# A pace of 0.56 instead of 0.46 for the S5 set-up in the last two token-major stages, and one more step in the mLSTM gates

## The chip, the cores and the metric

One core of a Trainium2 chip runs the whole program. Its engines work side by side, each through its own instruction queue in a fixed order, and wait for one another by semaphores: PE (TensorE, the matmuls), DVE (VectorE), ACT (ScalarE), POOL (GpSimd), and SP, which issues most of the DMA transfers. PE writes into eight PSUM banks, each of which another engine must read out before PE may use it again. The metric is the device time of one execution in microseconds (us), the median of several; lower is better.

## The reference, cut to what matters

One layer: an input projection of 1024 tokens, three mixers on its column groups (S5, mLSTM, SSD), an output projection and a LayerNorm.

```python
h = jnp.einsum('bld,dn->bln', x, w_in[l])          # 1024 x 2048 times 2048 x 6676
(s5_u, s5_z, ml_qk, ml_v, ml_i, ml_f, ml_o, ml_z, ssd_xbc, ssd_dt, ssd_z) = split_in(h)
y_s5 = s5_mixer(s5_u, ...) * silu(s5_z)            # diagonal complex state space, 32 groups x 64 states
y_ml = mlstm_mixer(q, k, ml_v, ml_i, ml_f, ml_o, ...) * silu(ml_z)   # gated matrix memory, 4 heads
y_ssd = rms_norm(ssd_mixer(...) * silu(ssd_z), ssd_norm_g)
out = jnp.einsum('bln,nd->bld', concatenate([y_s5, y_ml, y_ssd]), w_out[l])
x = layer_norm(DEEPNORM_ALPHA * x + out, ln_g[l], ln_b[l])
```

In `s5_mixer` the matrices that depend on the parameters alone (`lam_bar`, `b_bar`, the powers of `lam_bar`) can be formed before any token is known: that is the S5 set-up. In `mlstm_mixer` the running maximum of the gates, `m_row`, is needed for `exp(-m_row)` in the denominator: that is what the second edit moves.

## The kernel before

Every float32 operand is split into a high and a low part (`split`, L170 to L172: ACT casts the high part, DVE subtracts it for the low part), and each product is three matmuls: high by high, high by low, low by high.

The first part of the program, `block`, computes some column groups of the input projection by a recursive two-by-two scheme with seven products numbered 1 to 7. It has a token-major part (tokens on the partitions) in five stages, (1), (2), (5, 6), (3, 7) and (4). In each stage there are three column groups g = 0, 1, 2, of 512, 404 and 512 columns; each product of a group takes four units u, and one unit is 24 matmuls, which finish four PSUM banks named `b<i><g><t>` (product, group, token tile t) after the fourth unit. In stages (1), (2), (3, 7) and (4) all four banks come from one pool of four, `pj`: the next group writes the same four banks. In units 0 and 3 the matmuls run tile by tile, so that the banks finish, and are needed again, one after the other. `evac_t` reads a finished bank out with the additions of L1298 on DVE (tiles `e...`, named like the banks); product 7 has two such additions for a bank.

A column-major part follows (`b<i>c<g>`, L1443 to L1445), then for each half of the tokens the stage `half` with the projections for mLSTM and SSD and the mixers themselves, and at last `outproj`.

Work that is not on this main line is written as Python generators and handed to `Background`. Each unit ends with a `tick`, which adds the rate of the first generator in the list to an accumulator and runs one step of the generator (up to its next `yield`) for each whole number reached. The S5 set-up, `s5_setup`, is one such generator with 29 steps: 12 of small arithmetic, then two steps for each of eight blocks `sb`, and a last one. The first step of a block makes `s5lb`, `s5ob` (six 128x512 DVE products with helpers `s5l2`, `s5o2`) and writes `s5ob` to DRAM; the second makes `s5ta` (three more, with helper `s5tb`), writes it out, and calls `read_out(sb-1)`: four PE transposes `s5R` and four matmuls `s5K` of the tile `s5lb`, an ACT copy `s5rr`, a DVE addition `s5kb`, and two more writes. They use the other PSUM pool, `mx`. The set-up runs at rate 0.31 up to stage (3, 7), then at the rate that the diff changes; what is left after the last stage is run at once by `bg.finish(setup)`.

By these rates, of the 84 ticks of the token-major part (stage (3, 7) is ticks 49 to 72, stage (4) 73 to 84), 13 steps are done at tick 48. With 0.46 step 29 falls on tick 83; with 0.56 on tick 77, and the generator is closed at tick 79. The accumulator then passes 0.38 on to the next generator, the S5 mixer `s5_mix`, where it was 0.58.

The order in which steps are called is not the order of the queues: a scheduler between this code and the engines places the instructions of all steps by priorities and expected readiness. So the queues themselves are shown below.

In `half`, the generator `pre` runs `gates`, `cumulate` and `ml_gates` at rate 1.5. `ml_gates` ends with a part behind two yields: the four PE transposes `mg0mt` (L608) of the running maximum `mg0m`, which a DVE scan (L589) makes, and the ACT exponential of it. The main line at that place is `proj_c`, the products `qk0_0p`, `qk0_1p`, `qk0_2p`, each 48 matmuls with two weight tiles (`w125` and `w126` for the second, `w127` and `w128` for the third). Behind `pre` the generators `ml_mix`, `ml_finish` and `ssd_super` run.

Of the kernel before, what the change touches and what calls it, by code (L numbers as in the profile page):

```python
# [39 lines left out]
def hybrid_trunk(ctx: ExitStack, tc: tile.TileContext, a: dict, out: bass.AP, dbg=None):  # L40
# [15 lines left out]
    def gt(name, shape=(P, HT), dtype=F32):  # L56
        return gp.tile(list(shape), dtype, name=name, tag="g")

    def pm(name):
        return mx.tile([P, HT], F32, name=name, tag="mx")  # L60
# [106 lines left out]
    bg = Background()  # L167
# [417 lines left out]
    def ml_gates(h, G, NC, b, lf, ir, res):  # L585
        n = f"mg{h}"

        m = gt(n + "m", (4, HT))
        dve.tensor_tensor_scan(out=m, data0=lf, data1=ir, initial=mcar, op0=ALU.add, op1=ALU.max)  # L589
        mst = sp.tile([4, 4], F32, name=n + "mst", tag="mst")  # L590
        pool.tensor_copy(out=mst[:, 0:1], in_=mcar)
        pool.tensor_copy(out=mst[:, 1:4], in_=m[:, P - 1:3 * P:P])
        pool.tensor_copy(out=mcar, in_=m[:, HT - 1:HT])
        A = gt(n + "A", (4, HT))
        dve.tensor_tensor(out=A, in0=b, in1=m, op=ALU.subtract)
        sync.dma_start(out=rowd[h][12:16], in_=A)
        A2 = gt(n + "A2", (4, HT))
        ms = mst.unsqueeze(2).to_broadcast([4, 4, P])
        dve.tensor_tensor(out=A2.rearrange("p (c k) -> p c k", k=P), in0=A.rearrange("p (c k) -> p c k", k=P), in1=ms, op=ALU.add)
        sync.dma_start(out=rowd[h][16:20], in_=A2)  # L600

        Bj = sp.tile([P, 4, 4], F32, name=n + "Bj", tag="mBj")
        dve.tensor_tensor(out=Bj, in0=G[:, :, 16:20], in1=NC[:, :, 32:36], op=ALU.add)
        yield
        yield
        mt = pm(n + "mt")
        for c in range(4):
            pe.transpose(mt[:, 4 * c:4 * c + 4], m[:, c * P:(c + 1) * P], ident[0:4, 0:4])  # L608
        em = sp.tile([P, 16], F32, name=n + "em", tag="mem")
        act.activation(out=em, in_=mt[:, 0:16], func=AF.Exp, scale=-1.0)  # L610
        res += [Bj, em]
# [608 lines left out]
    def aside_1():  # L1220

        for u in range(4):
            c = Chain(xq(0, 0, u), (P, 2, HT), f"xc{u}")
            c.mix(xq(1, 0, u), sub, False, xs[u][7])
            yield

    def aside_2(X5):

        for u in range(4):
            c = Chain(xq(1, 0, u), (P, 2, HT), f"xd{u}")  # L1230
            c.mix(xq(1, 1, u), add)
            X5.put(c.r)
            yield
            c.mix(xq(0, 0, u), sub, False, xs[u][6])
            yield

    def aside_3():

        for u in range(4):
            yield  # L1240
            c = Chain(xs[u][6], (P, 2, HT), f"xe{u}")
            c.mix(xq(0, 1, u), sub, True, xs[u][3])
            yield
            yield

    def aside_4():

        for u in range(4):
            yield
            yield  # L1250
            c = Chain(xq(1, 0, u), (P, 2, HT), f"xf{u}")
            c.mix(xq(1, 1, u), add, False, xs[u][5])
            yield
# [31 lines left out]
    def block():  # L1285
# [78 lines left out]
        def unit(i, X, g, u, ps, w):  # L1364
            wh, wl = w
            N = GN[g]
            order = [(t, k) for t in range(4) for k in range(2)] if u == 3 or u == 0 and (i, g) != (1, 0) else [(t, k) for k in range(2) for t in range(4)]
            for t, k in order:
                K = 2 * u + k
                s_h, s_l = X.h[u][:, k, t * P:(t + 1) * P], X.l[u][:, k, t * P:(t + 1) * P]  # L1370
                pe.matmul(ps[t][:, 0:N], lhsT=s_h, rhs=wh[:, k, :], start=(K == 0), stop=False)
                pe.matmul(ps[t][:, 0:N], lhsT=s_h, rhs=wl[:, k, :], start=False, stop=False)
                pe.matmul(ps[t][:, 0:N], lhsT=s_l, rhs=wh[:, k, :], start=False, stop=(K == 7))  # L1373
                if K == 7:
                    evac_t(i, g, t, ps[t])
            tick()

        def banks(i, g, p):
            return [p.tile([P, HT], F32, name=f"b{i}{g}{t}", tag="pj" if p is pj else "mx") for t in range(4)]
# [6 lines left out]
        def ahead(sg, g, i, u):  # L1386

            if sg == (1,) and g == 1:
                ops[2].load(u)
            elif sg == (2,) and g == 2:  # L1390
                ops[6].load(u)
            elif sg == (5, 6) and (g, i) == (2, 6):
                ops[3].load(u)
                ops[7].load(u)
            elif sg == (3, 7) and (g, i) == (2, 3):
                ops[4].load(u)
            elif sg == (4,) and g == 1:
                cops[5].load(u)
            elif sg == (4,) and g == 2:
                cops[6].load(u)  # L1400

        for sg in STAGES:
            if sg == (2,):
                aside.append(aside_2(ops[5]))
            if sg == (5, 6):
                aside.append(aside_3())
            if sg == (3, 7):
                aside.append(aside_4())
                bg.q = [(q, 0.46) for q, _ in bg.q]
            for g in range(3):  # L1410
                if sg == (5, 6):
                    ps = {5: banks(5, g, pj), 6: banks(6, g, mx)}
                    for u in range(4):
                        w = [W.next(), W.next()]
                        for i, w_ in zip(sg, w):
                            unit(i, ops[i], g, u, ps[i], w_)
                        ahead(sg, g, 6, u)
                else:
                    for i in sg:
                        ps = banks(i, g, pj)  # L1420
                        for u in range(4):
                            if (i, g) == (1, 0):
                                first.load(u)
                            unit(i, ops[i], g, u, ps, W.next())
                            ahead(sg, g, i, u)
                if sg == (1,) and g == 0:
                    aside.append(aside_1())
# [52 lines left out]
    def half(h, X, Xn):  # L1480
# [4 lines left out]
        def pre():  # L1485
            G = Gs[:, h]
            DT, LC = gates(h, G)
            yield
            yield
            NC, b, lf, ir = cumulate(h, LC)  # L1490
            gx.extend([DT, NC])
            yield
            yield from ml_gates(h, G, NC, b, lf, ir, mlg)
# [117 lines left out]
    with tc.tile_pool(name="gb", bufs=NGB) as gp, tc.tile_pool(name="rb", bufs=NRB) as rw, tc.tile_pool(name="zp", bufs=NZ) as zp:  # L1611

        warm = gt("warm", dtype=BF16)
        dve.memset(warm, 0.0)
        wps = mx.tile([P, HT], F32, name="warmp", tag="mx")
        for _ in range(NWARM):
            pe.matmul(wps, lhsT=warm[:, 0:P], rhs=warm, start=True, stop=True)
        X[0] = block()
# [101 lines left out]
```

## Time and profile before

| quantity | value |
|---|---|
| time, median of 3 runs (lowest to highest) | 1613.33 us (1608.36 to 1613.99) |
| the profiled execution, its own time | 1613.81 us |
| its span, first to last instruction | 1612.1 us |
| DVE busy | 1123.4 us (70%) |
| ACT busy | 662.3 us (41%) |
| POOL busy | 79.7 us (5%) |
| HBM read, written | 271.74 MB, 57.28 MB |

The profile is of one execution. Its times start at the first instruction of the span. A row of the timeline gives the start, the duration, the engine, the line of the kernel, the operation, the tile written and the tiles read (buffer numbers mostly left out), how many were merged, and in brackets how long the engine had been idle and what ended the wait. Matmuls overlap, so that the time between two starts, not the duration in the row, is what one costs. A row of the windows view gives for a stretch of time its length, and for PE, the weight loads, DVE, ACT and POOL the busy time and the number of instructions, then the granted PE clock (1.00 is full), the share of the DMA engines in use and GB/s.

### The profile page before, as it was taken

The numbers are of one execution on the slowest core, as the hardware profiler recorded it, in microseconds if no ns is written. First come the engines' busy times: TensorE is split into PE (matmuls) and PEld (weight loads), VectorE is DVE, ScalarE is ACT, GpSimd is POOL, SyncE is SP. The second block draws the span as 40 slices with busy tenths as digits, with TensorE's granted clock in tenths as the row PEclk, the third lists the DMA queues.
The fourth block names the chain that finished last, engine by engine and source line by source line (L and its number), as shares of the span: only waits on it lengthen the run. The fifth ranks groups of instructions, "written<-read, shape, count | busy, mean of one in ns | idle before, by whom it ended". The sixth has DMA issues, their size and how long they took to land. (4 is left out here: it accounts for less than half of the span.)

```text
span 1612.1 us, 21150 instructions
## 1 busy us (share of the span) xinstructions
PE 1580.8 (98%) x7688; PEld 1331.6 (83%) x7688; DVE 1123.4 (70%) x1844; ACT 662.3 (41%) x929; POOL 79.7 (5%) x183
## 2 busy tenths in 40 slices
PE   9999999998999999999999999999999999999996
PEld 7898988987988888878888878888787888888884
DVE  5679978877878796564646887686697753484348
ACT  4333242236445556542542546365354331321221
POOL 0000000000011200010100000011001000000000
PEclk9999999999999999999999999999999999999998
DMA  8898777987897768363435544452654453565445
GB/s 315 318 324 332 259 255 257 310 277 239 290 343 243 249 219 284 132 227 120 147 96 164 193 154 124 144 171 63 215 188 146 138 185 120 187 233 161 129 144 182
DMA packets 139303, 333.56 MB, mean 207 GB/s; under 512 B 24488, under 2 KB 41000, under 8 KB 139200
## 3 DMA queue, kind: packets, MB, share of 16 engines
q1 hardware_dynamic: 129792, 317.54, 58.9%
q10 hardware_dynamic: 9408, 14.68, 2.7%
q8 instruction: 60, 0.98, 0.2%
q14 instruction: 43, 0.35, 0.1%
HBM read 271.74 MB, written 57.28 MB: 204 GB/s over the span
## 5 line engine op out<-in xcount | busy, mean ns | idle before, releaser
L1298 DVE TENSOR_TENSOR e<-e,b 128x512 f32<-128x512 f32 (+1 forms) x72 | 43.7, 646 | 5.0 <-PE b L1373 4.9
L1557 DVE SCALAR_TENSOR_TENSOR r<-r,mv,ln_g 128x512 f32<-128x512 f32 x32 | 23.1, 740 | 0.0
L1558 DVE SCALAR_TENSOR_TENSOR r<-r,lrs,ln_b 128x512 f32<-128x512 f32 x32 | 22.9, 740 | 0.0
L363 ACT ACT_TABLE_LOAD x16 | 20.5, 1283 | 3.0 <-DVE qc00cv L362 2.8
L1577 DVE BATCH_NORM_STATS2 bst<-r 128x6 f32<-128x512 f32 x32 | 21.2, 684 | 0.0
L1053 POOL COPY s5m0up<-s5m0u 128x256 f32<-128x256 f32 x2 | 2.5, 1253 | 309.1 <-DMA s5m0u<-s5u 309.1
L172 DVE TENSOR_TENSOR y1l<-y1r,y1h 128x1024 fp32r<-128x1024 f32 x8 | 9.8, 1221 | 8.1 <-ACT y1h L171 8.1
L1278 ACT ACTIVATE f<-f 128x512 f32<-128x512 f32 x20 | 12.1, 626 | 3.3 <-DVE f L1298 2.5
L1549 ACT ACTIVATE lrs<-lrs 128x1 f32<-128x1 f32 x8 | 1.6, 202 | 26.8 <-DVE lrs L1548 26.8
L171 ACT CAST y1h<-y1r 128x1024 fp32r<-128x1024 f32 x8 | 8.4, 1052 | 9.7 <-PE op03p L345 9.7
L171 ACT CAST x1h<-x1r 128x1024 fp32r<-128x1024 f32 x8 | 8.4, 1046 | 9.2 <-PE xbc_13p L1532 9.2
L172 DVE TENSOR_TENSOR y0l<-y0r,y0h 128x1024 fp32r<-128x1024 f32 x8 | 9.8, 1220 | 3.0 <-ACT y0h L171 3.0
L780 DVE TENSOR_TENSOR s5small<-s5small 128x32 f32<-128x32 f32 (+2 forms) x66 | 11.3, 194 | 0.7
L172 DVE TENSOR_TENSOR x1l<-x1r,x1h 128x1024 fp32r<-128x1024 f32 x8 | 9.8, 1220 | 2.3 <-ACT x1h L171 2.2
L742 PEld LDWEIGHTS mf<-ident,sgo 128*128 128x128 f32 x48 | 5.5, 140 | 6.3 <-DVE sgo L732 5.6
L171 ACT CAST y0h<-y0r 128x1024 fp32r<-128x1024 f32 x8 | 8.3, 1043 | 5.6 <-PE xbc_13p L1532 5.6
L1298 DVE TENSOR_TENSOR f<-f,b1c 128x512 f32<-128x512 f32 x15 | 9.4, 681 | 1.6 <-ACT f L1351 1.6
L730 DVE SCALAR_TENSOR_TENSOR sgo<-m1hm,m1nd,sgo 128x192 f32<-128x192 f32 x16 | 5.9, 414 | 6.5 <-DMA sgo<-og 6.5
L742 PE MATMUL mf<-ident,sgo 128*128 128x128 f32 x48 | 9.0, 283 | 1.5 <-DVE sgo L732 1.3
L732 DVE TENSOR_TENSOR sgo<-sgo,mzs 128x384 f32<-128x384 f32 x16 | 8.9, 556 | 2.1 <-DMA mzs<-zg 1.8
L1272 ACT ACT_TABLE_LOAD x8 | 10.3, 1283 | 0.1
L676 DVE SCALAR_TENSOR_TENSOR st_m<-st_m,m1dec,m1o 96x193 f32<-96x193 f32 x12 | 4.9, 408 | 6.8 <-PE m1o L672 6.7
(4696 smaller groups left out, 5744.8 us busy)
## 6 DMA issues: line engine op xcount, KB each, us to landing
xn<-in_x_dram SPq DMA_DIRECT2D x32, 256.0 KB, 5.5
out_dram<-r SPq DMA_DIRECT2D x32, 256.0 KB, 3.4
x1r<-in_xT_dram SPq DMA_DIRECT2D x8, 512.0 KB, 3.6
y0r<-mixT SPq DMA_DIRECT2D x8, 512.0 KB, 4.1
y1r<-mixT SPq DMA_DIRECT2D x8, 512.0 KB, 3.6
vd<-e SPq DMA_DIRECT2D x16, 192.0 KB, 4.0
szd<-f ACTq DMA_DIRECT2D x12, 256.0 KB, 2.0
vx<-vd SPq DMA_DIRECT2D x8, 384.0 KB, 4.3
```

What stands on the lines that cost most here:

```text
L171: act.copy(out=th, in_=raw)
L172: dve.tensor_sub(out=tl, in0=raw, in1=th.bitcast(F32))
L363: act.activation(out=dest, in_=c, func=AF.Silu)
L732: dve.tensor_mul(out=sg, in0=sg, in1=sz)
L742: pe.transpose(pt[:, c * P:(c + 1) * P], hg[c][t // 3][:, (t % 3) * P:(t % 3 + 1) * P], ident)
L780: eng.tensor_tensor(out=o, in0=i, in1=j, op=op)
L1272: act.activation(out=c[:, 256:512], in_=c[:, 256:512], func=AF.Sigmoid)
L1278: act.activation(out=c, in_=c, func=AF.Silu)
L1298: dve.tensor_tensor(out=o, in0=x, in1=y, op=op)
L1557: dve.scalar_tensor_tensor(out=o, in0=o, scalar=mv[:, 0:1], in1=lng[nb], op0=ALU.subtract, op1=ALU.mult)
L1558: dve.scalar_tensor_tensor(out=o, in0=o, scalar=rs, in1=lnb[nb], op0=ALU.mult, op1=ALU.add)
L1577: dve.bn_stats(out=st[t][:, nb, :], in_=r[t][nb])
```

## The change

The rate of the S5 set-up in stages (3, 7) and (4) goes from 0.46 to 0.56 steps a tick, and `ml_gates` waits for three yields instead of two before its PE transposes.

```diff
@@ -601,6 +601,7 @@
         Bj = sp.tile([P, 4, 4], F32, name=n + "Bj", tag="mBj")
         dve.tensor_tensor(out=Bj, in0=G[:, :, 16:20], in1=NC[:, :, 32:36], op=ALU.add)
+        yield
         yield
         yield
         mt = pm(n + "mt")
@@ -1406,7 +1407,7 @@
             if sg == (3, 7):
                 aside.append(aside_4())
-                bg.q = [(q, 0.46) for q, _ in bg.q]
+                bg.q = [(q, 0.56) for q, _ in bg.q]
             for g in range(3):
```

No instruction is added or left out: the queues hold the same work in another order. Three places are shown; a number behind an underscore is the buffer's, and lines of the change stand one lower from the first edit on.

**The end of group 0 of stage (4), on DVE.** `e100` to `e103` read out the banks `b400` to `b403`, which group 1 needs next; `w76l` to `w78l` are the low parts of group 1's weights. Before:

```order
L172 TENSOR_TENSOR w76l_3626<-w76r_3620,w76h_3625 128x808
L1298 TENSOR_TENSOR e100_325<-e100_325,b400_3506 128x512
L172 TENSOR_TENSOR w77l_3675<-w77r_3669,w77h_3674 128x808
L780 TENSOR_TENSOR s5kb4_3503<-s5K4_3498,s5dd_605 128x64
L780 TENSOR_TENSOR s5lb6_3609<-s5small2_1182,s5bb1_1485 128x512
L780 TENSOR_TENSOR s5l26_3610<-s5small5_1608,s5bb2_1486 128x512
L780 TENSOR_TENSOR s5ob6_3614<-s5small2_1182,s5c1s_1606 128x512
L780 TENSOR_TENSOR s5lb6_3609<-s5lb6_3609,s5l26_3610 128x512
L780 TENSOR_TENSOR s5o26_3615<-s5small3_1335,s5c2_600 128x512
L1298 TENSOR_TENSOR e101_333<-e101_333,b401_3507 128x512
L172 TENSOR_TENSOR w78l_3736<-w78r_3730,w78h_3735 128x808
```

In the change, directly behind `w77l` and `s5kb5`:

```order
L781 TENSOR_TENSOR s5lb7_3576<-s5small2_1182,s5bb1_1485 128x512
L781 TENSOR_TENSOR s5l27_3577<-s5small5_1608,s5bb2_1486 128x512
L781 TENSOR_TENSOR s5ob7_3581<-s5small2_1182,s5c1s_1606 128x512
L781 TENSOR_TENSOR s5lb7_3576<-s5lb7_3576,s5l27_3577 128x512
L781 TENSOR_TENSOR s5o27_3582<-s5small3_1335,s5c2_600 128x512
L781 TENSOR_TENSOR s5ta7_3653<-s5afr_1911,s5f1_2262 128x512
L781 TENSOR_TENSOR s5ob7_3581<-s5ob7_3581,s5o27_3582 128x512
L172 TENSOR_TENSOR w78l_3785<-w78r_3779,w78h_3784 128x808
L781 TENSOR_TENSOR s5tb7_3654<-s5a2_2264,s5f2_2263 128x512
L781 TENSOR_TENSOR s5kb6_3672<-s5K6_3667,s5dd_605 128x64
L781 TENSOR_TENSOR s5ta7_3653<-s5ta7_3653,s5tb7_3654 128x512
L1299 TENSOR_TENSOR e100_325<-e100_325,b400_3539 128x512
```

`e100`, which stood ahead of `w77l` and of all of the set-up's products there, now stands behind `w77l`, `w78l` and both steps of the last block. `e101`, `e102` and `e103` follow it directly. On PE, the last read-out of the set-up, `s5R7` and `s5K7`, now stands between `b403` and `b410`, where nothing stood before.

**The end of stage (3, 7), on DVE.** `e520`, `e120` and their like read out the banks `b720` to `b723`, which stage (4) needs; on PE two read-outs of the set-up stand between the two stages, before and in the change. Before:

```order
L223 TENSOR_TENSOR w76r_3620<-w76r_3620,w76q0_3622 128x808
L780 TENSOR_TENSOR s5kb3_3304<-s5K3_3299,s5dd_605 128x64
L172 TENSOR_TENSOR w73l_3516<-w73r_3510,w73h_3515 128x1024
L780 TENSOR_TENSOR s5lb5_3383<-s5small2_1182,s5bb1_1485 128x512
L172 TENSOR_TENSOR p43l_3310<-p43r_3307,p43h_3309 128x1024
L780 TENSOR_TENSOR s5l25_3384<-s5small5_1608,s5bb2_1486 128x512
L780 TENSOR_TENSOR s5ob5_3388<-s5small2_1182,s5c1s_1606 128x512
L780 TENSOR_TENSOR s5lb5_3383<-s5lb5_3383,s5l25_3384 128x512
L780 TENSOR_TENSOR s5o25_3389<-s5small3_1335,s5c2_600 128x512
L172 TENSOR_TENSOR w74l_3549<-w74r_3543,w74h_3548 128x1024
L780 TENSOR_TENSOR s5ob5_3388<-s5ob5_3388,s5o25_3389 128x512
L1298 TENSOR_TENSOR e520_2327<-e520_2327,b720_3313 128x512
```

In the change:

```order
L223 TENSOR_TENSOR w76r_3675<-w76r_3675,w76q0_3677 128x808
L781 TENSOR_TENSOR s5kb4_3337<-s5K4_3332,s5dd_605 128x64
L172 TENSOR_TENSOR w73l_3549<-w73r_3543,w73h_3548 128x1024
L781 TENSOR_TENSOR s5lb6_3416<-s5small2_1182,s5bb1_1485 128x512
L172 TENSOR_TENSOR p43l_3343<-p43r_3340,p43h_3342 128x1024
L781 TENSOR_TENSOR s5l26_3417<-s5small5_1608,s5bb2_1486 128x512
L781 TENSOR_TENSOR s5ob6_3421<-s5small2_1182,s5c1s_1606 128x512
L781 TENSOR_TENSOR s5lb6_3416<-s5lb6_3416,s5l26_3417 128x512
L781 TENSOR_TENSOR s5o26_3422<-s5small3_1335,s5c2_600 128x512
L1299 TENSOR_TENSOR e520_2327<-e520_2327,b720_3346 128x512
L172 TENSOR_TENSOR w74l_3593<-w74r_3587,w74h_3592 128x1024
L781 TENSOR_TENSOR s5ob6_3421<-s5ob6_3421,s5o26_3422 128x512
```

The block's number is one higher and `e520` stands two rows earlier; its partner `e120`, without which the bank is not free, comes next behind `s5ob` in both.

**The transposes of the mLSTM gates, on PE.** Before:

```order
L300 MATMUL qk0_1p_6454<-p23l_5864,w126h_6457 128x512
L301 MATMUL qk0_1p_6454<-p23h_5863,w126l_6458 128x512
L608 MATMUL mg0mt_6542<-ident_73,mg0m_6485 128x4 x4
L299 MATMUL qk0_2p_6549<-p10h_5434,w127h_6501 128x512
L300 MATMUL qk0_2p_6549<-p10l_5435,w127h_6501 128x512
```

In the change:

```order
L300 MATMUL qk0_2p_6542<-p13l_5615,w127h_6501 128x512
L301 MATMUL qk0_2p_6542<-p13h_5614,w127l_6502 128x512
L609 MATMUL mg0mt_6573<-ident_73,mg0m_6485 128x4 x4
L299 MATMUL qk0_2p_6542<-p20h_5705,w128h_6545 128x512
L300 MATMUL qk0_2p_6542<-p20l_5706,w128h_6545 128x512
```

They stand 24 matmuls later, behind the first half of the third projection. The scan that makes `mg0m` keeps its place on DVE.

Elsewhere the read-outs of blocks 0 to 3 stand earlier on PE in stage (3, 7) (the first by 24 matmuls). At the end of that stage's group 0, DVE has nine of block 2's products ahead of `e500`, where one stood ahead of it. In the column-major part some matmuls of the S5 mixer stand one block of 24 later. In both halves some of the mLSTM's score and chunk matmuls stand 24 to 60 rows earlier or later, and the place of `mg1mt` in the second half is the same.

## The prediction

> **What bounds the kernel now.** I read the busy times first, then PE's waits, then the stretches around the two longest with the granted clock.
>
> ```profile
> PE 1580.8 (98%) x7688; PEld 1331.6 (83%) x7688; DVE 1123.4 (70%) x1844; ACT 662.3 (41%) x929; POOL 79.7 (5%) x183
> PE s5R L985 <- DVE s5lb L780: 2.3, 1, 2.3
> PE b L1371 <- DVE e L1298: 1.9, 1, 1.9
> PE s01xt L434 <- DVE s01dx L435: 1.7, 1, 1.7
> PE mg0mt L608 <- DVE mg0m L589: 1.6, 1, 1.6
> ```
>
> PE is busy for 98% of the span, and a wait row gives the microseconds in total, the count and the longest. No row exceeds 2.3 us. A change that only reorders can move the time by these waits, by new ones, and by the clock that follows them. Three of the four longest concern the edit: `s5R` and `b` stand together at the end of stage (3, 7), and `mg0mt` is the second edit's place.
>
> ```profile
> 383.10 0.63 PE L985 MATMUL s5R<-ident,s5lb 128*128 128x128 f32 x4 [2.27 <-DVE s5lb L780]
> 386.54 0.79 PE L1371 MATMUL b<-w72h,p40h 128*128 128x512 f32 x1 [1.95 <-DVE e L1298]
> 391.38 0.40 PE L1373 MATMUL b<-w72h,p40l 128*128 128x512 f32 x1
> 387.90:391.40 3.50, 3.50 (x10) 2.65 (x9) 3.50 (x6) 3.07 (x5) 0.00 (x0) 0.51 0.31 111
> 391.40:394.80 3.40, 3.40 (x16) 2.80 (x15) 3.40 (x5) 1.55 (x3) 0.00 (x0) 1.00 0.26 51
> ```
>
> Event 1 is a read-out that waits 2.27 us for its tile, a bank that waits 1.95 us, and then half clock: the windows rows show 0.51 up to 391.4 and 1.00 behind it. From 386.54 to 391.38 matmuls start eleven steps apart. Full speed is 0.227 us each (six from 409.31 to 410.67 in the rows of stage (4) below), 2.5 us in all, so 4.84 - 2.5 = 2.3 us go to the clock. Event 1 costs 2.27 + 1.95 + 2.3 = 6.5 us.
>
> ```profile
> 719.61 1.27 DVE L589 TENSOR_TENSOR_SCAN mg0m<-cu0lf,mcar,cu0ir 4x512 f32<-4x512 f32 x1 [0.92 <-ACT cu0ir L415]
> 720.94 0.41 PE L608 MATMUL mg0mt<-ident,mg0m 4*128 4x4 f32 x4 [1.63 <-DVE mg0m L589]
> 722.31 0.50 PE L300 MATMUL qk_2p<-p10l,w127h 128*128 128x512 f32 x1
> 725.96 0.39 PE L300 MATMUL qk_2p<-p12l,w127h 128*128 128x512 f32 x1
> 722.40:725.90 3.50, 3.50 (x10) 2.75 (x9) 3.39 (x5) 1.50 (x3) 1.75 (x3) 0.51 0.39 110
> ```
>
> Event 2 is the same in small: 1.63 us of waiting for the scan, then one stretch at clock 0.51. From 722.31 to 725.96 it is nine steps, 3.65 us instead of 2.0, so 1.6 us are lost. Event 2 costs 3.2 us.
>
> **The second edit.** The transposes move 24 matmuls on, 24 x 0.227 = 5.4 us. PE, freed at 720.94 - 1.63 = 719.31, runs the first half of `qk0_2p` at once and reaches them at 724.76. The scan ends at 719.61 + 1.27 = 720.88, 3.9 us earlier. Next late could be the low parts for those matmuls:
>
> ```profile
> 710.98 1.23 DVE L172 TENSOR_TENSOR w127l<-w127r,w127h 128x1024 fp32r<-128x1024 f32 x1 [0.86 <-ACT w127h L171]
> 717.46 1.23 DVE L172 TENSOR_TENSOR w128l<-w128r,w128h 128x1024 fp32r<-128x1024 f32 x1 [3.81 <-ACT w128h L171]
> ```
>
> `w127l` is ready at 712.2, `w128l` at 718.7, both before use. So the wait goes and with it the clock's drop: **-3.2 us** (bounds 0, if the wait only finds another place, and -3.2).
>
> **The end of stage (3, 7).** The first edit should have its gain here, and I count nothing. The order shows the same DVE rows for a block one higher: the six products still stand ahead of the rows that free the bank, and the PE read-out that needs `s5lb` still stands between the stages. The DVE rows do not start by the tick that called them:
>
> ```profile
> 377.14 1.00 DVE L223 TENSOR_TENSOR w76r<-w76r,w76q 128x808 f32<-128x808 f32 x1 [2.35 <-DMA w76q<-in_w_gv_dram]
> 382.26 0.69 DVE L780 TENSOR_TENSOR s5lb<-s5lb,s5l 128x512 f32<-128x512 f32 x1
> ```
>
> They run without a gap behind `w76r`, which waits for a DMA, and that DMA and its row remain. Hence `s5lb` again ends near 382.9. `e520` is two rows earlier, but `e120`, which frees the bank, is not. **0 us**, bounds -6.5 (both waits go) and +1.5.
>
> **The end of group 0 of stage (4).** Here I see the cost. Before:
>
> ```profile
> 405.43 0.87 ACT L171 CAST w77h<-w77r 128x808 fp32r<-128x808 f32 x1 [0.88 <-PE b L1373]
> 406.79 0.69 DVE L1298 TENSOR_TENSOR e<-e,b 128x512 f32<-128x512 f32 x1 [4.10 <-PE b L1373]
> 407.40 1.00 DVE L172 TENSOR_TENSOR w77l<-w77r,w77h 128x808 fp32r<-128x808 f32 x1
> 408.31 0.22 DVE L780 TENSOR_TENSOR s5kb<-s5K,s5dd 128x64 f32<-128x64 f32 x1
> 408.44 0.68 DVE L780 TENSOR_TENSOR s5lb<-s5small,s5bb 128x512 f32<-128x512 f32 x1
> ...
> 411.45 0.68 DVE L1298 TENSOR_TENSOR e<-e,b 128x512 f32<-128x512 f32 x1
> ...
> 414.76 1.14 DVE L780 TENSOR_TENSOR s5ta<-s5afr,s5f 128x512 f32<-128x512 f32 x1
> ...
> 416.81 1.26 DVE L172 TENSOR_TENSOR p51l<-p51r,p51h 128x1024 fp32r<-128x1024 f32 x1
> 409.31 0.39 PE L1371 MATMUL b<-w75h,p43h 128*128 128x512 f32 x1
> 410.67 0.34 PE L1371 MATMUL b<-w76h,p40h 128*128 128x404 f32 x1
> 433.76 0.60 PE L985 MATMUL s5R<-ident,s5lb 128*128 128x128 f32 x4
> 435.01 0.47 PE L1371 MATMUL b<-w81h,p41h 128*128 128x512 f32 x1
> ```
>
> Row 406.79 is `e100`: DVE had idled 4.10 us for its bank, and it was out at 407.4, long before PE wanted the bank at 410.67. In the change `e100` stands behind twelve other rows from `w77l` on. They may start when `w77h` is cast, 405.43 + 0.87 = 406.30. By the distances between starts above they cost: `w77l` 0.91, `s5kb` 0.13, five products 3.01 (408.44 to 411.45), `ta` and `tb` 2.05 (414.76 to 416.81), `ob` 0.60 like each of the five, `w78l` 0.91 like `w77l`, another `s5kb` 0.13, the last addition of `ta` 0.60: 8.34 us. So `e100` starts at 414.7 and ends, with its 0.69, at 415.4. PE reaches the group at 410.67 plus the read-out that now stands there, 435.01 - 433.76 = 1.25: 411.92. That 1.25 is moved from 433.76, not added. The bank is late by 415.4 - 411.92 = 3.5 us. The other evacuations follow directly, 0.6 us apart, faster than PE asks. By events 1 and 2, half clock follows such a wait: 2.3 and 1.6 us there; I take 1.5 us for one stretch begun partly idle. **+5.0 us.** Bounds: 0, if `e100` is not held, and 3.5 plus two stretches, some 2.8, which is 6.3.
>
> **The end of group 0 of stage (3, 7).** Eight more products stand ahead of `e500` here.
>
> ```profile
> 285.95 0.99 DVE L172 TENSOR_TENSOR w56l<-w56r,w56h 128x808 fp32r<-128x808 f32 x1
> 290.04 1.23 DVE L223 TENSOR_TENSOR xf2r<-xf2r,xf2q 128x1024 f32<-128x1024 f32 x1 [3.09 <-DMA xf2q<-in_xT_dram]
> 291.18 0.99 DVE L172 TENSOR_TENSOR w57l<-w57r,w57h 128x808 fp32r<-128x808 f32 x1
> 298.62 0.68 DVE L1298 TENSOR_TENSOR e<-e,b 128x512 f32<-128x512 f32 x1
> 299.90 0.34 PE L1371 MATMUL b<-w56h,p30h 128*128 128x404 f32 x1
> ```
>
> DVE's idle 3.09 us covers part of them: from 286.85 they take 0.13 + 3.01 + 2.05 + 0.60 = 5.8, to 292.6. `xf2r` (1.14) and `w57l` (0.91) end at 294.7, seven evacuations at 0.60 at 298.9, `w58l` (0.91) at 299.8, and the last one, at 298.62 before, is over at about 300.5. PE takes up that group at 299.90. **+0.6 us**, bounds 0 and +4.4 (a 3.0 us wait and 1.4 of clock).
>
> **The rest: 0.** SP's queue now has two S5 writes of the first read-out ahead of a load of weights, and must wait there for `s5kb`:
>
> ```profile
> 285.10 0.45 SPq L209 DMA_DIRECT2D w58r<-in_w_gv_dram  x1
> 296.80 0.88 ACT L171 CAST w58h<-w58r 128x808 fp32r<-128x808 f32 x1 [5.43 <-PE b L1373]
> ```
>
> By the DVE rows `s5kb` is done near 287.1, so `w58r` is issued about 2 us later than 285.10; its cast comes 11.7 us after that issue and waits for PE, so the delay is covered. On PE the S5 mixer's and mLSTM's matmuls only change places with others, and PE stays full. If one of them comes too early for its operand, it costs about what the third wait row showed, 1.7 us; I keep that to both sides.
>
> **Sum.** 1613.81 - 3.2 + 0 + 5.0 + 0.6 = 1616.2 in the terms of the profiled execution, which lay 0.5 above the median: **1615.7, rounded to 1616 us.**
>
> **The rivals.** What a measurement of this kernel can tell from no change is about 0.5%, 8 us: faster is below 1605.3, slower above 1621.4.
>
> *The new wait stays hidden*: DVE reaches the rows of stage (4) before 403, and `e100` is in time. For it speaks that some of the work is now earlier; against it, that `w77l` and `w78l` wait for ACT's casts, which wait for PE (0.88 above). 1613.8 - 3.2 + 0.6 - 0.5 = 1610.7.
>
> *The set-up's waits go as well*, event 1 and no new one: 1610.7 - 6.5 = 1604.2. Against it is the unchanged order there.
>
> *The change doesn't do what it says*: the transposes only carry their wait along, because the scan slips too. 1613.8 + 5.0 + 0.6 - 0.5 = 1618.9. Against it: the scan's place on DVE is the same and the margin 3.9 us.
>
> *Slower*: DVE's backlog also closes the bank at the end of group 0 of stage (3, 7). If the products there start 3.4 us later than 286.85, the last evacuation ends at 303.9, PE waits 4.0 and loses 1.4 of clock, 5.4 instead of 0.6; with the upper end at stage (4), 6.3, the sum is 1613.8 - 3.2 + 5.4 + 6.3 - 0.5 = 1621.8. It decides from a delay of 3 us on. For it speaks the thin margin, against it the idle 3.09 us.
>
> [...]
>
> **How the numbers follow.** Forecast 0.50; new wait hidden 0.15; clock unmoved 0.08; wait carried along 0.09; all waits gone 0.09; both groups late 0.09. The last two lie beyond the 0.5%, so faster 0.10, same 0.80, slower 0.10. The range takes in the other cases with their bounds: 1610.7 less 1.7 and less part of event 1's gain, 1607.5, up to 1621.
>
> **What would show it.** In the changed profile: `mg0mt` no longer waits, and the clock is 1.00 around 722 to 726. The waits for `s5lb` and `e` remain at about 383 and 386, with half clock to 391. A new PE wait of about 3.5 us for an `e` of L1299 stands near 415, perhaps split with the read-out ahead of it, and 1.5 us of half clock behind. Near 300 a wait under 1 us. The forecast is wrong if `e100` starts before 412, or if event 1 is gone.

## The result and the profile after

| | time, us | of before |
|---|---|---|
| before, median of 4 on the chips of this pair | 1611.76 (1608.36 to 1613.99) | |
| changed | 1622.78 (1621.84 to 1623.80) | 1.0078, interval 1.0065 to 1.0091 |
| before, medians beside the experiments (29, 20, 22 runs) | 1609.8, 1608.9, 1608.8 | |

The change makes the kernel slower by 0.8%, some 12.5 us. (A ratio, here and below, comes with its 95% interval; it is not the quotient of the two medians, which here is 1.0068.) The profiled execution of before, on which the forecast was built (1613.81 us), is itself some 4 to 5 us above the medians of 20 and more runs; so the 1616 us that the forecast named was only 2.4 us above its own base.

The view of PE's waits after the change (microseconds in total, count, longest), its first three rows:

```profile
PE b L1372 <- DVE e L1299: 5.5, 4, 3.3
PE s5m6U L1060 <- POOL s5m5X L1088: 4.8, 1, 4.8
PE s5R L986 <- DVE s5lb L781: 2.4, 1, 2.4
```

The row of `mg0m` is gone and so is the second half's 1.7 us for `s01dx`. The wait for a bank of 3.3 us is new, and so is a wait that the forecast didn't know: 4.8 us in the S5 mixer.

Where the difference arises is read from the starts of the same matmul in both traces. Before:

```profile
283.65 0.39 PE L1371 MATMUL b<-w53h,p71h 128*128 128x512 f32 x1
309.25 0.34 PE L1371 MATMUL b<-w58h,p32h 128*128 128x404 f32 x1
378.68 0.39 PE L1371 MATMUL b<-w71h,p73h 128*128 128x512 f32 x1
409.99 0.39 PE L1371 MATMUL b<-w75h,p43h 128*128 128x512 f32 x1
427.69 0.35 PE L1371 MATMUL b<-w79h,p43h 128*128 128x404 f32 x1
452.13 0.39 PE L1371 MATMUL b<-w83h,p43h 128*128 128x512 f32 x1
640.33 0.39 PE L1443 MATMUL b1c<-p13h,w112h 128*128 128x512 f32 x1
```

After:

```profile
283.51 0.39 PE L1372 MATMUL b<-w53h,p71h 128*128 128x512 f32 x1
312.71 0.34 PE L1372 MATMUL b<-w58h,p32h 128*128 128x404 f32 x1
382.15 0.39 PE L1372 MATMUL b<-w71h,p73h 128*128 128x512 f32 x1
413.23 0.39 PE L1372 MATMUL b<-w75h,p43h 128*128 128x512 f32 x1
438.57 0.34 PE L1372 MATMUL b<-w79h,p43h 128*128 128x404 f32 x1
460.24 0.39 PE L1372 MATMUL b<-w83h,p43h 128*128 128x512 f32 x1
655.97 0.39 PE L1444 MATMUL b1c<-p13h,w112h 128*128 128x512 f32 x1
```

Each stretch's length after, less its length before, less 1.25 us for a read-out that now lies in it, gives:

| place | forecast | in these two traces |
|---|---|---|
| end of group 0, stage (3, 7) | +0.6 | 29.20 - 25.60 - 1.25 = +2.3 |
| event 1, end of stage (3, 7) | 0 | 31.08 - 31.31 = -0.2 |
| end of group 0, stage (4) | +5.0 | 25.34 - 17.70 - 1.25 = +6.4 |
| column-major part | 0 | 195.73 - 188.20 = +7.5 |

The four add up to 16.0 us, and at the end of the column-major part the change is 655.97 - 640.33 = 15.6 us behind. The spans differ by 1622.0 - 1612.1 = 9.9: the halves give some 6 us back. 2.6 of it lie between the start of the first projection and the second half of the third, where the transposes stand (the change is 15.6 us behind at the one and 13.05 at the other); the rest is spread over the second half, and the traces of the experiments are shorter there than this one of before by 1 to 4 us too, with the step or without it.

**The end of group 0 of stage (4)** went as forecast, in its order and its wait. DVE and PE after the change, and PE's windows there (length, busy time and count of PE, weight loads, DVE, ACT and POOL, then the granted clock):

```profile
409.57 1.00 DVE L172 TENSOR_TENSOR w77l<-w77r,w77h 128x808 fp32r<-128x808 f32 x1 [3.53 <-ACT w77h L171]
417.85 2.48 DVE L1299 TENSOR_TENSOR e<-e,b 128x512 f32<-128x512 f32 x4
414.35 0.96 PE L995 MATMUL s5K<-s5c1s,s5lb 128*128 128x64 f32 x8
418.58 0.70 PE L1372 MATMUL b<-w76h,p40h 128*128 128x404 f32 x1 [3.27 <-DVE e L1299]
418.40:421.80 3.40, 3.22 (x10) 3.16 (x11) 3.40 (x7) 1.87 (x4) 0.00 (x0) 0.50 0.97 371
421.80:425.20 3.40, 3.40 (x13) 3.34 (x12) 2.06 (x2) 0.54 (x1) 0.00 (x0) 0.56 1.05 317
425.20:428.60 3.40, 3.40 (x20) 3.40 (x19) 1.58 (x2) 0.87 (x1) 0.40 (x1) 1.00 0.99 359
```

From `w77l` to `e100` are 8.28 us (8.34 were added up), and PE waits 3.27 (3.5). But the half clock reaches over two stretches (0.50 and 0.56, then 1.00), not one.

**The wait in the S5 mixer.** The wait row names a memset of POOL. The rows of the queues tell what was really late. SP after; SP before, with PE's matmul before, which had no wait; then POOL and PE after, PE's two windows behind, and the longest row of SP's waits after, between 560 and 590:

```profile
568.93 0.38 SPq L209 DMA_DIRECT2D w104r<-cg  x1
576.78 0.33 SPq L209 DMA_DIRECT2D w104q<-in_w_c_dram  x1
578.89 0.98 SPq L1051 DMA_DIRECT2D s5m6u<-s5u  x2
```

```profile
559.13 0.98 SPq L1050 DMA_DIRECT2D s5m6u<-s5u  x2
569.44 0.34 SPq L209 DMA_DIRECT2D w104q<-in_w_c_dram  x1
571.69 0.60 PE L1059 MATMUL s5m6U<-ident,s5m6up 128*128 128x128 f32 x4
```

```profile
584.38 4.30 POOL L1054 COPY s5m6up<-s5m6u 128x256 f32<-128x256 f32 x2 [23.26 <-DMA s5m6u<-s5u]
588.62 0.10 POOL L1088 MEMSET s5m5X<- 128x4 f32 x1
588.73 1.11 PE L1060 MATMUL s5m6U<-ident,s5m6up 128*128 128x128 f32 x4 [4.79 <-POOL s5m5X L1088]
587.40:590.80 3.40, 2.07 (x7) 1.88 (x8) 1.82 (x2) 0.25 (x1) 2.39 (x4) 0.68 1.00 387
590.80:594.20 3.40, 3.40 (x13) 2.71 (x13) 1.39 (x3) 0.00 (x0) 0.00 (x0) 0.81 0.47 109
SPq L209 <- DVE p40l L172: 7.4, 1, 7.4
```

Before, SP issued the load of `s5m6u` ahead of `w104q`; after, behind it. `w104q` must wait for its buffer (7.4 us, for `p40l`), and `s5m6u` waits in the queue with it: 578.89 instead of 559.13. POOL's copies of it end at 588.7, and PE, free at 588.73 - 4.79 = 583.94, waits for them; the memset only happens to end last. The rest of the 7.5 us is the lowered clock behind it (0.68 and 0.81) and smaller waits.

**The transposes** wait no more (`mg0mt` at 741.10 has no bracket), and the clock is 1.00 there.

### The profile page after: what moved, and what is told of

Its sections match the earlier page's. It is cut to its first block, busy times and chain, and to the rows that moved or that the text cites. A ratio compares the mean times of both kernels' runs of the same rounds, so it can differ in the third digit from the quotient of the medians.

```text
span 1622.0 us, 21177 instructions
## 1 busy us (share of the span) xinstructions
PE 1583.8 (98%) x7688; PEld 1333.5 (82%) x7688; DVE 1124.1 (69%) x1844; ACT 659.4 (41%) x927; POOL 81.0 (5%) x183
## 5 line engine op out<-in xcount | busy, mean ns | idle before, releaser
L1307 ACT COPY e<-b 128x512 f32<-128x512 f32 (+1 forms) x12 | 6.7, 557 | 7.3 <-PE b L1374 7.3
```

## The experiments

In each, before ran beside it; ratios are of before. 0.001 is 1.6 us.

### The S5 mixer: the accumulator, and one load's place

The only thing of the pace that the code carries into the column-major part is the remainder in the accumulator. The changed kernel with the old remainder:

```diff
         bg.finish(setup)
+        bg.acc = 0.58
         gT, gs = [], ([], [])
```

> The changed kernel, with the accumulator set to 0.58 where the S5 mixer is added, its value in the kernel before (the change leaves 0.38). Theory (the 0.38 lets the scheduler put two weight loads ahead of the load of s5m6u on SP's queue, and that is the 4.8 us wait in the S5 mixer and its half clock): the wait of s5m6U goes and the time falls by 6 to 7.5, to about 1616 us; the waits near 302, 386 and 418 stay. Rival (the wait comes from the earlier set-up itself, its writes or its work on DVE): no change, 1622.8 us.

Measured: 1613.34 us, 1.0034 (1.0021 to 1.0046). The wait of `s5m6U` is gone, and the matmuls of the column-major part are in the order of before; the 3.27 us at `b<-w76h` and the waits near 301 and 386 stand. Against 1.0078 this is 7.1 us. The other way round, the kernel before with `bg.acc = 0.38` at that line:

> The kernel before, old pace and all, with the accumulator set to 0.38 instead of 0.58 where the S5 mixer is added; PE's order in the column-major part is then that of the changed kernel. Theory (the accumulator alone makes the wait in the S5 mixer): a PE wait of some 4.8 us for POOL before s5m6U near 575 to 580 and the time 6 to 7.5 above before, about 1617 us. Rival (the earlier set-up is needed for it): within 2 us of before, 1608 to 1612.

Measured: 1615.64 us, 1.0043 (1.0031 to 1.0055), 6.9 us slower. PE's order in the column-major part and its row are the same as after the change, with nothing else of the change in the kernel:

```profile
579.65 1.12 PE L1059 MATMUL s5m6U<-ident,s5m6up 128*128 128x128 f32 x4 [4.79 <-POOL s5m5X L1087]
```

Last, the changed kernel with 0.38, but with that one load moved (`ld_u` is the load of `s5m6u` as it was, called two steps earlier; the mixer's block 6 takes the tiles from `ub6`, and its matmuls then stand a little earlier on PE too; the line that moves it):

```diff
+        if sb == 5:
+            ub6.append(ld_u("s5m6", 3))
         A = pm(n + "b")
```

> The changed kernel with its accumulator of 0.38, but s5m6u is loaded two steps of the S5 mixer earlier, so that on SP it stands ahead of w104q and w105r. Theory (the load's place behind w104q, which waits for its buffer, is the cause): the wait at s5m6U goes, 6 to 7.5 us below the changed kernel, about the time of the run with the accumulator kept, 1613 us. Rival (POOL or DVE work of the mixer is late by itself): the wait stays within 1 us, about 1620 us.

Measured: 1613.91 us, 1.0026 (1.0016 to 1.0035), 8.4 us below 1.0078. SP issues the load 9 us ahead of `w104q`, and PE does not wait there:

```profile
563.73 1.07 SPq L1053 DMA_DIRECT2D s5m6u<-s5u  x2
572.44 0.33 SPq L209 DMA_DIRECT2D w104q<-in_w_c_dram  x1
```

The three agree within their intervals, 2 to 3 us each: some 7 of the 12.5 us come from a remainder of 0.38 that puts one load behind another that waits. The earlier set-up itself has no part in it, nor has the extra step, which the second run doesn't have.

### The end of group 0 of stage (4): row order, and what the clock follows

On the run with the accumulator kept, the evacuations of that group at high priority:

```diff
                 if K == 7:
-                    evac_t(i, g, t, ps[t])
+                    with tc.high_priority() if (i, g) == (4, 0) else nullcontext():
+                        evac_t(i, g, t, ps[t])
```

> The run with the accumulator kept, and besides the evacuations of group 0 of stage (4) at high priority, so that e100 stands right behind w77l on DVE and not behind the last block of the set-up. Theory (that row order is the whole cost at the end of that group, 3.3 us of waiting and 3.1 of half clock): the wait near 418 goes and the time is 6.4 below the run with the accumulator kept, about 1609.5 us. Rival (w78l or the read-out s5R7 is late in its place and PE waits there): 1613 to 1616 us, with a new PE wait between 412 and 430.

Measured: 1608.47 us, 0.9995 (0.9985 to 1.0005): 6.3 us below its neighbour. `e100` follows `w77l`, and PE goes over the border without a bracket:

```profile
413.67 0.39 PE L1374 MATMUL b<-w75h,p43l 128*128 128x512 f32 x1
413.90 0.34 PE L1372 MATMUL b<-w76h,p40h 128*128 128x404 f32 x1
```

So that row order is the whole cost of the place, as far as these runs tell. How much of it is clock? Again on the run with the accumulator kept, PE is first given work in its wait:

```diff
-            for g in range(4):
+            for g in list(range(4)) * (5 if sb == 7 else 1):
                 gg = 4 * sb + g
```

> The run with the accumulator kept, and the four matmuls of the last read-out, s5K7, run five times over (the same values written again), so that PE works through most of the 3.3 us that it waits for e100. Theory (the half clock behind 418 is the price of PE's idleness, about 3.1 us): the bank wait falls under 0.5 us, the clock stays 1.00 between 415 and 425, the time is 2 to 3 below the run with the accumulator kept, about 1610.5 us. Rival (the clock falls there for another reason): same as the run with the accumulator kept, 1613.3 us, or up to 0.5 above it.

Measured: 1614.26 us, 1.0042 (1.0025 to 1.0059), no gain. The bank wait is gone, and PE is busy without a gap, yet the clock falls to 0.50, for one stretch:

```profile
412.34 4.55 PE L995 MATMUL s5K<-s5c1s,s5lb 128*128 128x64 f32 x40
413.30:416.70 3.40, 3.40 (x33) 3.40 (x33) 3.40 (x7) 2.13 (x4) 0.00 (x0) 1.00 0.62 178
416.70:420.10 3.40, 3.40 (x12) 3.36 (x12) 3.40 (x6) 2.08 (x4) 0.00 (x0) 0.50 0.99 378
```

These matmuls are 16 to 64 columns wide. The same with four of 512 columns:

```diff
             ps = pm(f"s5K{sb}")
+            for _ in range(4 if sb == 7 else 0):
+                pe.matmul(ps, lhsT=lb[:, 0].rearrange("p s c -> p (s c)"), rhs=f3(lb), start=True, stop=True, skip_group_check=True)
```

> The run with the accumulator kept, and four float32 matmuls of 128x512 ahead of the last read-out's own (their result is overwritten), in the place where PE waits 3.3 us for e100. Busy with narrow matmuls of 16 to 64 columns there PE still fell to half clock, for one stretch instead of two. Theory (the clock follows how much of its time PE spends on wide matmuls): no half clock between 412 and 426, and 1.5 to 3 below the run with the accumulator kept, 1610.5 to 1612 us where before stands at 1609. Rival (the clock falls there whatever PE does): half clock again for one or two stretches behind 416, and 1613 to 1614.5 us.

Measured: 1612.81 us, 1.0024 (1.0011 to 1.0036). The time doesn't settle it (its interval overlaps that of 1.0034, without any work in the wait); the clock of the profiled execution stays at 1.00:

```profile
415.00:418.40 3.40, 3.40 (x13) 1.73 (x11) 3.40 (x6) 2.87 (x4) 0.00 (x0) 1.00 0.36 107
418.40:421.80 3.40, 2.92 (x16) 2.54 (x15) 3.40 (x6) 1.79 (x3) 0.00 (x0) 1.00 0.88 317
```

So the half clock there seems to go with what PE does in those 3.3 us. In all four traces with the 3.27 us wait (the change, the pace alone, the accumulator kept, the load moved) the clock falls behind it, for one stretch or two (in the change 0.50 and 0.56). With matmuls of 16 to 64 columns in that place it fell to 0.50 as well, and with four of 512 ahead of them it stayed at 1.00, in one execution of each; what the clock costs there in time was not measured.

### The extra step

One line of the change alone, in the kernel before:

```diff
+        yield
         yield
         yield
         mt = pm(n + "mt")
```

> The kernel before with the extra step and the old pace of 0.46. Theory (the costs add up): 1611.8 - 3.2 = about 1608.5 us, no PE wait for mg0m, clock 1.00 around 722 to 726. Rival (the gains in the second half belong to the step): about 1605 us, with the wait of s01xt at 963 gone too. Second rival (a wait of the same size only moves): 1611.8 us.

Measured: 1606.05 us, 0.9984 (0.9972 to 0.9995), 2.6 us less, and once more 0.9989 (below). The traces show why the gain is not simply the wait at `mg0mt`. In the execution profiled here, one of the longest of the twelve (1610.14 us), that wait is gone, but PE waits 1.98 us for `gt1f` at 709.55, where before had no wait, with a clock of 0.50 behind it, and the three projections take as long as before (0.3 us more). In the profile of the second run that wait is 0.54, and they take 2.7 us less. And the pace alone, `0.56` without the step:

> The kernel before with the pace of 0.56 and without the extra step. Theory (the costs add up place by place): everything that the change cost stays and only the gain at the transposes goes, so 1622.8 + 3.3 = about 1626 us, with the wait of 1.6 us for mg0m back and the 4.8 us wait of s5m6U unchanged. Rival (the gains in the second half of the tokens, some 3.5 us, come from the extra step as well): about 1629.5 us, with the wait of s01xt near 1.7 us back too. Second rival (the extra step causes the wait in the S5 mixer): about 1618 us.

Measured: 1621.22 us, 1.0077 (1.0058 to 1.0096): level with the whole change. All three theories missed. Beside the pace the step has little to save, as its wait is short there even without it:

```profile
733.59 0.41 PE L608 MATMUL mg0mt<-ident,mg0m 4*128 4x4 f32 x4 [0.68 <-DVE mg0m L589]
```

The kernel before with 0.38 shows the same 0.68 us. Both have the long wait in the S5 mixer ahead, which therefore isn't the step's doing. Why the scan is less late behind it stays open.

### Event 1, and a version that beats both kernels

The extra step at the old pace, with the evacuations of (7, 2) and (4, 0) at high priority, by the same edit with `(i, g) in ((7, 2), (4, 0))`:

> The extra step with the old pace, and the evacuations at the end of stage (3, 7) and of group 0 of stage (4) at high priority: they stand ahead of the set-up's products on DVE, and one PE read-out fewer stands between the stages. Theory (event 1 is a matter of DVE's row order there): both waits of event 1 and their half clock go, 6.5 us below the extra step alone, about 1599.5 us. Rival (the products only crowd the next group, e100 or w77l is late then): 1604 to 1607 us with a new PE wait between 405 and 440.

Measured: 1605.56 us, 0.9984 (0.9975 to 0.9994), level with the step alone. The wait for `s5lb` is gone, but set-up work put off from there comes up at the end of group 1:

```profile
425.63 0.47 PE L1372 MATMUL b<-w80h,p40h 128*128 128x512 f32 x1 [1.84 <-DVE e L1299]
```

With (4, 1) at high priority too:

> The extra step, old pace, and at high priority the evacuations at the end of stage (3, 7) and of groups 0 and 1 of stage (4); in the run with two of them the wait had moved to the end of group 1 (1.84 us at 425.6), behind the set-up's products and w81l. Theory (DVE's row order there again): that wait falls to under 0.8 us and the time is 1 to 2 below the extra step alone on this chip, about 0.9970 of before. Rival (the work put off is late once more, or the place is not worth what the profile says): level with the extra step alone, 0.9984 of before.

Measured: 1604.11 us, 0.9965 (0.9953 to 0.9977); that wait falls from 1.84 to 0.86 us. Beside it on the same chip, the step alone:

> The extra step alone once more, beside the run with three sets of evacuations first, since the two lay on different chips and their ratios within each other's intervals. Theory (event 1 costs its 6.5 us in every execution): this run is 5 to 7 us slower than its neighbour. Rival (its removal is worth little, for what PE gains there it loses at later waits that are bound to DVE or DMA): within 2 us of its neighbour.

Measured: 1607.08 us, 0.9989 (0.9977 to 1.0000), 3 us slower than its neighbour: between the theory and its rival. Two executions of this one kernel show why event 1 has no fixed price. First the earlier run, then this one, each with PE's two waits there and a window:

```profile
384.39 0.63 PE L986 MATMUL s5R<-ident,s5lb 128*128 128x128 f32 x4 [2.25 <-DVE s5lb L781]
387.84 0.80 PE L1372 MATMUL b<-w72h,p40h 128*128 128x512 f32 x1 [1.86 <-DVE e L1299]
387.60:391.00 3.40, 3.16 (x8) 2.50 (x9) 3.40 (x7) 2.97 (x5) 0.00 (x0) 0.50 0.61 218
```

```profile
383.47 0.63 PE L986 MATMUL s5R<-ident,s5lb 128*128 128x128 f32 x4 [1.30 <-DVE s5lb L781]
386.91 0.50 PE L1372 MATMUL b<-w72h,p40h 128*128 128x512 f32 x1 [1.95 <-DVE e L1299]
387.00:390.40 3.40, 3.40 (x15) 2.82 (x16) 3.40 (x7) 2.97 (x5) 0.00 (x0) 1.00 0.54 197
```

The second waits are alike, the first are not, and one execution fell to half clock (0.50) while the other stayed at 1.00. In the first it had fallen by 385.7 already (a mean of 0.72 from 384.20 to 387.60), before the second wait was over. But with waits of 1.15 and 1.96 us, much like those of the second execution, the run with the load moved fell to half clock as well, for one stretch:

```profile
388.60:392.00 3.40, 3.40 (x10) 2.63 (x9) 3.40 (x6) 2.98 (x4) 0.00 (x0) 0.50 0.62 222
```

Pace and step as in the change, with the accumulator at 0.58 and the evacuations of (7, 0), (7, 2) and (4, 0) at high priority:

> The changed kernel with its accumulator kept at 0.58 and the evacuations of stage (3, 7), groups 0 and 2, and of group 0 of stage (4) at high priority: pace and step as in the change, its two large waits and event 1 taken out. Theory (the costs add up): what is left is the step's gain of 2.6, event 1's 6.5 and 2 lost near 300, so about 7 below before, 0.9956. Rival (set-up work put off from one end shows up at the next, as with the old pace): 0.998 to 1.001 of before, with a PE wait of over 1.5 us between 395 and 450.

Measured: 1604.63 us, 0.9966 (0.9953 to 0.9978), and a wait of 1.29 us at 429.8. Both mended versions beat both kernels, by about 5.5 us and 18 us, and in neither trace is there a stretch of half clock between 12 and 1590 us (the mean granted clock is 0.996 and 0.997 over these executions, 0.993 over the one of before). They come out level, with different paces and different evacuations put first.

## Why the prediction was wrong, point by point

- **The end of group 0 of stage (4)**: right in place, cause, row count and wait (3.27 for 3.5). The term was 1.4 us too small, since I took one stretch of half clock, where two followed; the two were in the upper bound, 6.3. The clock did fall at the new wait, so the case of an unmoved clock (0.08) did not come. (The last read-out came from 446.0, not from 433.76; one at each place moved ahead, and the size is the same.)
- **"The rest: 0"** is the step that failed. It said that on PE the S5 mixer's matmuls only change places and PE stays full. I had looked at PE's order there, and at SP's queue only around `w58r`; the order of SP in the column-major part, where `s5m6u` falls behind `w104q`, I did not follow. PE stood idle there for 4.79 us and went on at a lowered clock (0.68 and 0.81). It was worth +7.5 us in the trace and about 7 by three runs, against the ±1.7 that I allowed.
- **The end of group 0 of stage (3, 7)**: right in sign, +2.3 for +0.6, within its bounds. The chain on DVE started later and had a wait for a buffer in it, as its rows after the change show:

```profile
287.53 0.22 DVE L781 TENSOR_TENSOR s5kb<-s5K,s5dd 128x64 f32<-128x64 f32 x1
291.35 1.14 DVE L781 TENSOR_TENSOR s5ta<-s5afr,s5f 128x512 f32<-128x512 f32 x1 [0.59 <-DMA s5R<-s5rr]
297.52 0.42 PE L1372 MATMUL b<-w56h,p30h 128*128 128x404 f32 x1 [0.90 <-ACT w58h L171]
301.92 0.45 PE L1372 MATMUL b<-w56h,p30h 128*128 128x404 f32 x1 [0.75 <-DVE e L1299]
```

  I had it start at 286.85 and followed the last bank alone; the first one was late too. (The row at 297.52 names a cast; with the accumulator kept, the same matmul waits 1.13 us for `e`.) No run undid this place by itself.
- **Event 1**: right, both waits stayed (2.44 and 1.20 us). That it costs 6.5 us holds for that execution only, and the half clock did not come behind both waits: before, the granted clock is 0.50 from 384.5 to 387.9 already, while the second wait is on.
- **The extra step**: right in sign alone (-2.6 and -1.8 us by its two runs, the second up to the edge of no change, for -3.2), wrong in company: beside the pace it saved nothing that could be measured, so the terms do not add up.
- **The base**: the sum was made on an execution some 4 us above the kernel's median. No other execution of before was traced, but of its two waits of 1.6 us and more in the halves (`mg0m`, `s01dx`) the kernel with 0.38, which has the same order there, shows only 0.68 and 1.0 us. Single executions of before lie half a per cent apart (1605.09 to 1613.85 us in 29); three runs gave no sure base, while the medians beside the experiments agree within 1 us.

The slower rival came out at 1621.8, near the time measured, but by another mechanism; it gets no credit.

## What to carry to other kernels

When a pace or a rate is changed, follow its remainder: the work behind it shifts as well, and the queue to read there is the one that waits in order (here SP, where one load that waited 7.4 us for a buffer held up the load behind it). A wait row can name a bystander, as the memset here; look for the copy or the DMA ahead of it. And before costs of a few microseconds are added up, see whether several executions show them; evacuations that free a bank PE needs next are worth a priority of their own.

## What the runs showed of the hardware

- Waits that are alike were followed by half clock in one execution and by full clock in another: behind 1.15 and 1.96 us at event 1 the clock was 0.50 for one stretch, behind 1.30 and 1.95 us it stayed at 1.00. Within the one execution of before, a wait of 1.63 us (event 2) had a clock of 0.51 behind it, while around one of 1.68 us it was 1.00:

```profile
963.21 0.55 PE L434 MATMUL s01xt<-ident,xc 128*128 128x128 f32 x3 [1.68 <-DVE s01dx L435]
959.50:966.50 7.00, 5.32 (x34) 4.43 (x33) 6.94 (x11) 2.15 (x3) 0.18 (x1) 1.00 0.68 190
```

- In the traces of before and of the change the clock is 1.00 from 12 to 1590 us, but for five times at 0.50. Before, these last 6.83 us at event 1 and 3.41 us at event 2; after, 6.83 us at event 1, 6.83 us behind the wait of 3.27 us and 3.41 us behind that of 4.79 us in the S5 mixer. What sets these lengths was not shown.
- PE's busy share alone did not keep the clock up. In one execution PE was busy for 4.4 us with matmuls of 16 to 64 columns, and the clock fell to 0.50 for a stretch; in another, with four matmuls of 512 columns ahead of the narrow ones, it stayed at 1.00. It also stayed there with matmuls of 128 columns: in before, 56 of the 58 matmuls in this window have 128 columns (tile `s01y`), and the clock is 1.00 in it and in the 3.4 us behind it:

```profile
1012.60:1016.00 3.40, 3.40 (x58) 3.15 (x58) 3.33 (x13) 0.63 (x1) 0.19 (x1) 1.00 0.42 141
```
